# Reordering the opening stage of a two-block transformer kernel: loads, squares, first weights and PSUM banks

## The chip, the cores and the metric

The kernel runs on one NeuronCore of one Trainium2 chip. The core has five engines with a queue of instructions each: TensorE (PE in the profile, with its weight loads as PEld), VectorE (DVE), ScalarE (ACT), GpSimd (POOL) and SyncE (SP, which here only issues DMAs). Each queue runs in its own order and waits on semaphores of the others. The metric is the device time of one execution in microseconds; less is better.

## The reference, cut to what matters

Two transformer blocks run one after the other on one sequence of 512 tokens of width 1024, all in float32. What concerns the opening stage is the modulated norm at the entry of block 1, its first two projections, and the keys and values of a 256-row memory, which block 2 needs much later but which depend on nothing in block 1.

```python
mod = c @ w_ada + b_ada                                  # c is one row of 1024
shift, scale, gate = jnp.split(mod, 3, axis=-1)
h = _rmsnorm(x, norm_g) * (1.0 + scale[:, None, :]) + shift[:, None, :]
proj = h @ w_in                                          # q_a, k_a, v_a, z_a, q_b, ...
...
kv = jnp.einsum("bmd,de->bme", rmsnorm(mem, norm_mem_g), w_ckv)   # in block 2's cross attention
```

## The kernel before

**Number format.** Every large product is float32 built from three matmuls: weights and activations are split into a high part (fp32r) and a low part (the rest). For a weight tile of 128 x 1024 that is a cast on ScalarE (L166, `wh`) and a subtraction on VectorE or GpSimd (L167, `wl`); a string of letters (`START_LO`, D or P for each unit) says which. A "unit" is such a tile, 0.5 MiB in memory; it is loaded into `wr` (three buffers), and its two halves go into `wh` and `wl` (three buffers each).

**The front.** The first stage stands in a block whose order is written out by hand for all engines (`manual_schedule`): each engine runs its instructions in the order of the code. A loop over n = 0 to 9 runs ten units of the memory's keys (n = 0 to 7) and values (8, 9) on TensorE, 24 matmuls of 256 columns each, while block 1's input is prepared beside them. Around each unit stand: the squares of x (`squares_x`: ScalarE squares, one engine adds into `xacc`), the loads and the products of the modulation (`ada_load` reads one of 16 rows of tiles `ar`, and `ada` multiplies it with the broadcast row c in PSUM, `cb`, and sums along the row on VectorE; ScalarE then makes `shift` or `gain` of it), the copy of a finished unit to `kvo` and from there to DRAM by a DMA of the GpSimd queue, and some matmuls on zeros (`spin`, counts in `SPINS`). At n = `NORM_AT` the column sums of `xacc` give the norm's factor: a short chain on VectorE and ScalarE (`rsq`, `bcast_split`), then a broadcast on TensorE into `xrb` (PSUM).

**The eight h tiles.** `token_h(j)` makes one 128 x 512 slice of block 1's input: `y` = x times gain times `xrb` on VectorE into a PSUM bank, its high part on ScalarE (with the shift as bias), its low part on VectorE. `H_AT` says after which n slice j comes. Before, all eight y share one bank (tag `idle`).

**Queues.** SyncE issues all loads. A load of `wr` waits until the unit three before it has been split; a load of `ar` (eight buffers) waits until the product eight before it is done; and each issue waits for the DMA eight before it to have landed. Behind the loop stand `memory_squares` (the norm of the memory) and eight stores of the memory's split (`ms_d`).

**After the front.** From block 1 on the order is made by a list scheduler from the program's order. Block 1 opens with `qk("qa", "ka", 0)`: two chunks of 24 matmuls of 512 columns with the weights of units qa:0 and ka:0 and all eight h slices, then four units of values (va, into the banks `z` and `lin`).

Of the kernel before, what the change touches and what calls it, by code (L numbers as in the profile page):

```python
# [17 lines left out]
P = 128  # L18
# [3 lines left out]
KD = 8  # L22
# [53 lines left out]

START_LO = "DDDPPPPPPP"
N_FRONT = 10  # L80
AR_BUFS = 8
SQ_AT = (0, 0, 1, 1, 2, 2, 3, 3)
ADA_LOADS = (2, 2, 2, 2, 2, 2)
ADA_AT = (1, 1, 2, 2, 3, 3, 4, 4, 5, 5, 6, 6, 7, 7, 8, 8)
NORM_AT = 4
H_AT = (6, 6, 7, 7, 8, 8, 9, 9)
SPINS = (0, 2, 2, 2, 2, 3, 3, 3, 3, 3)
B1_LO = "DP"
B2_LO = 23 * "P" + "DPPDPDPDPDP"

# [25 lines left out]
def block_kernel(ctx, tc, wts, vec, c_row, lam_v, cst, x_t, mem_t, pos, out):  # L116
# [53 lines left out]
    def unit(name, j, n=D):  # L170
        return split(load(UNITS[name] + j, n), n)
# [13 lines left out]
    def chunk(name, c, xs, ps_=None):  # L185
        o = (ps_ or ps_lin)()
        lin_k(o, unit(name, c), 0, xs)
        return o

    def tok(name, xs, parts=(0,), ps_=None):  # L190
# [181 lines left out]
    def memory_squares():  # L372
        for raw in raws:
            act.activation(out=raw, in_=raw, func=AF.Square)
        s = raws[0]
        dve.tensor_tensor(out=s, in0=s, in1=raws[1], op=ALU.add)
        dve.tensor_tensor(out=s[:, :T], in0=s[:, :T], in1=s[:, T:], op=ALU.add)
        dve.tensor_tensor(out=mrb, in0=s[:, :NM], in1=s[:, NM:T], op=ALU.add)

    raw_of, split_of = {}, {}

    def mem_load(n):
        if n < N_FRONT:
            raw_of[n] = load(UNITS["mk"] + n)

    def mem_split(n):
        if n < N_FRONT:
# [55 lines left out]
    def ada(i):  # L445
        r, j, m = ada_raw[i], i // 2, mod[:, i:i + 1]
        dve.scalar_tensor_tensor(out=r, in0=r, scalar=1.0, in1=cb, op0=ALU.mult, op1=ALU.mult, accum_out=m)
        if i % 2 == 0:
            act.activation(out=shift[:, j:j + 1], in_=m, func=AF.Identity, bias=V("b_shift", j))
        else:  # L450
            act.activation(out=gain[:, j:j + 1], in_=m, func=AF.Identity, scale=V("norm_g", j),
                           bias=gain0[:, j:j + 1])
# [4 lines left out]
    def squares_x(i):  # L457
        if i == 0:
            act.activation(out=xacc, in_=xt0[:, 0], func=AF.Square)
            return  # L460
        q = st.tile([P, T], F32, tag="xq", bufs=3, name="xq")
        act.activation(out=q, in_=xt0[:, i], func=AF.Square)
        dve.tensor_tensor(out=xacc, in0=xacc, in1=q, op=ALU.add)

    def token_h(j):

        sh = shift[:, j:j + 1]
        y = stp.tile([P, T], F32, tag="idle", bufs=1, name="y")
# [8 lines left out]
    with tc.manual_schedule(engines={E_.PE, E_.Activation, E_.DVE, E_.Pool, E_.SP}):  # L477
# [15 lines left out]
        memory(1)  # L493
        mem_load(0)
        mem_load(1)
        for k in range(0, KD, 2):
            load_x(k)
        mem_load(2)
        for _ in range(4):
            ada_load()  # L500
        mem_split(0)
        mem_split(1)
        spun[0] = ps_sm()
        rest = []
        for n in range(N_FRONT):
# [6 lines left out]
            mem_split(n + 2)  # L512
            out_ = mem_unit(n)
            spin(SPINS[n])
            if n == NORM_AT:
                for i in range(NT):
                    pe.matmul(xrb[:, i:i + 1], lhsT=xacc[:, i * P:(i + 1) * P], rhs=ones[:, 0:1], start=True, stop=True)
                rsq(xrc, xrb[:, :NT], D)
                xrs = bcast_split(xrc)
            if n == NORM_AT + 1:  # L520
                bcast_mm(xrs, xrb)
            for i in range(16):
                if ADA_AT[i] == n:
                    ada(i)
                    if rest:
                        rest.pop()()
            out_()
            for j in range(KD):
                if H_AT[j] == n:
                    while rest:  # L530
                        rest.pop()()
                    rest.append(token_h(j))
        rest.pop()()
        memory_squares()
        for i, t in enumerate(mt):
# [128 lines left out]

    def qk(qn, kn, c):
        qe, qo, ke, ko, kl = qkt = qk_tiles(ap, lows)
        q_stack(chunk(qn, c, hs), 0.125, qe, qo)
        k_stack(chunk(kn, c, hs), ke, ko, kl)
        return qkt

    def head_out(v, p, odd, tt, zs):
# [926 lines left out]
```

## Time and profile before

| | us |
|---|---|
| three runs, median (lowest to highest) | 1288.9 (1286.59 to 1288.98) |
| the profiled execution, device time | 1287.82 |
| its span, first to last instruction | 1286.0 |
| TensorE busy in the span | 1225.6 |
| mean granted clock of TensorE | 0.978 |

The profiled execution took 1287.82 us, of which 1.8 us lie outside the span of instructions; it stands 1.1 us below the median. Times below count from the span's start. A row of the timeline gives start and length in microseconds, engine, line, operation, output and inputs, how many instructions it merges, and in brackets the idle time of the engine ahead of it and what ended that. A row of windows gives the busy time of each engine in a stretch, the mean granted clock of TensorE (1.00 is the upper of its two levels, 2.4 GHz; 0.5 the lower, 1.2 GHz), the busy share of the DMA engines and the rate.

### The profile page before, as it was taken

Reading aid. Unit: us, or ns where it says so; the run is one execution under the profiler, and the core shown is the slowest. Engines: PE = TensorE matmul, PEld = TensorE weight load, DVE = VectorE, ACT = ScalarE, POOL = GpSimd, SP = SyncE. Lnnn points to the kernel's source line nnn. Section 1 sums busy time; section 2 is a strip of 40 time slices with the busy share of each in tenths; the row PEclk is TensorE's granted clock in tenths of the full one; section 3 lists DMA queues with packets and bytes.
Section 4 is the critical chain, followed back from the end, with each engine's and each line's share of the span. In section 5 each row is a group of like instructions: output and inputs, shape, how many; then the busy total and the mean of one; then the engine's idle time right before and its main releaser. Section 6 shows DMA issues by size and latency. Waiting matters only on the chain. (4 is left out here: it accounts for less than half of the span.)

```text
span 1286.0 us, 16873 instructions
## 1 busy us (share of the span) xinstructions
PE 1225.6 (95%) x6381; PEld 1031.9 (80%) x6381; DVE 779.6 (61%) x1242; ACT 599.4 (47%) x989; POOL 451.6 (35%) x302
## 2 busy tenths in 40 slices
PE   7899999999999999999988888999999999999997
PEld 5688888988887888888877776887888888888886
DVE  5865778665564274457767867456587777771113
ACT  4456565556633345256555355444444444442222
POOL 1463444322222238334635446104422222222221
PEclk8989999999999999999998998999999999999999
DMA  9833222232257343221342324212233333322222
GB/s 357 328 120 110 87 74 81 67 90 74 83 175 249 107 124 98 66 90 42 101 139 68 102 77 131 97 34 81 84 97 98 99 99 98 99 90 90 90 90 66
DMA packets 46018, 140.10 MB, mean 109 GB/s; under 512 B 5233, under 2 KB 8817, under 8 KB 45938
## 3 DMA queue, kind: packets, MB, share of 16 engines
q1 hardware_dynamic: 45170, 136.93, 33.2%
q0 software_dynamic: 768, 2.10, 0.4%
q8 instruction: 50, 0.82, 0.3%
q14 instruction: 30, 0.25, 0.1%
HBM read 127.48 MB, written 8.39 MB: 106 GB/s over the span
## 5 line engine op out<-in xcount | busy, mean ns | idle before, releaser
L148 PE MATMUL lin<-h,wh 128*128 128x512 f32 (+1 forms) x2232 | 693.5, 391 | 17.2 <-ACT wh L166 13.8
L148 PEld LDWEIGHTS lin<-h,wh 128*128 128x128 f32 x2232 | 417.7, 192 | 102.6 <-ACT wh L166 17.6
L148 PE MATMUL lin<-h,wl 128*128 128x512 f32 (+1 forms) x1116 | 434.7, 390 | 11.5 <-POOL wl L167 8.8
L167 POOL TENSOR_TENSOR wl<-wr,wh 128x1024 fp32r<-128x1024 f32 (+1 forms) x115 | 277.7, 2416 | 473.6 <-ACT wh L166 449.7
L166 ACT CAST wh<-wr 128x1024 fp32r<-128x1024 f32 (+1 forms) x197 | 204.6, 1040 | 255.0 <-PE lin L148 183.8
L148 PEld LDWEIGHTS lin<-h,wl 128*128 128x128 f32 x1116 | 214.2, 192 | 55.8 <-POOL wl L167 11.0
L167 DVE TENSOR_TENSOR wl<-wr,wh 128x1024 fp32r<-128x1024 f32 (+1 forms) x82 | 111.6, 1361 | 127.8 <-ACT wh L166 127.4
L148 PE MATMUL lin<-wh,h 128*128 128x256 f32 x672 | 128.8, 288 | 2.3 <-DVE h L1010 2.3
L148 PEld LDWEIGHTS lin<-wh,h 128*128 128x128 f32 x672 | 107.6, 193 | 3.1 <-issue 2.7
L1383 DVE SCALAR_TENSOR_TENSOR cv<-up,vecs,cv 128x512 f32<-128x512 f32 x88 | 94.2, 1071 | 18.3 <-ACT cv L1381 16.8
L148 PE MATMUL lin<-wl,h 128*128 128x256 f32 x336 | 96.1, 286 | 0.4 <-POOL wl L167 0.4
L148 PE MATMUL lin<-zz,wh 128*128 128x512 f32 (+1 forms) x324 | 92.3, 371 | 0.0
L148 PEld LDWEIGHTS lin<-zz,wh 128*128 128x128 f32 x324 | 58.5, 188 | 11.5
L148 PEld LDWEIGHTS lin<-wl,h 128*128 128x128 f32 x336 | 65.0, 194 | 1.0 <-POOL wl L167 0.7
L148 PE MATMUL lin<-zz,wl 128*128 128x512 f32 (+1 forms) x162 | 60.1, 371 | 0.0
L321 POOL TENSOR_TENSOR nacc<-nacc,sq 128x512 f32<-128x512 f32 x34 | 53.0, 1568 | 14.9 <-ACT sq L320 14.3
L1378 POOL MEMSET up<- 128x2 f32 x44 | 4.3, 99 | 148.5 <-DVE cv L1383 116.3
L683 POOL TENSOR_TENSOR zs<-zs,y 64x512 f32<-64x512 f32 x16 | 26.5, 1654 | 71.4 <-DVE y L682 69.8
L697 DVE TENSOR_TENSOR_SCAN om<-om 128x511 f32<-128x511 f32 (+3 forms) x32 | 35.9, 1162 | 9.5 <-ACT om L693 9.4
L1390 ACT ACTIVATE cv<-cv 128x512 f32<-128x512 f32 x22 | 13.9, 632 | 59.6 <-DVE cv L1383 59.6
L1379 DVE TENSOR_TENSOR up<-lin,rb 128x512 f32<-128x512 f32 x44 | 30.1, 686 | 16.1 <-PE lin L148 13.4
L218 DVE TENSOR_TENSOR tl<-z,th 128x512 fp32r<-128x512 f32 (+1 forms) x60 | 33.4, 595 | 9.5 <-ACT th L217 9.1
(406 smaller groups left out, 1715.6 us busy)
## 6 DMA issues: line engine op xcount, KB each, us to landing
wr<-in_wts SPq DMA_DIRECT2D x197, 512.0 KB, 3.5
ar<-in_wts SPq DMA_DIRECT2D x16, 512.0 KB, 9.4
qk<-qk SPq DMA_DIRECT2D x24, 128.0 KB, 2.3
wr<-in_wts SPq DMA_DIRECT2D x8, 384.0 KB, 3.0
xt<-in_x_t SPq DMA_DIRECT2D x4, 512.0 KB, 8.9
kv_d<-kvo POOLq DMA_DIRECT2D x16, 128.0 KB, 4.9
ms_d<-h SPq DMA_DIRECT2D x8, 256.0 KB, 6.2
ma_d<-gt SPq DMA_DIRECT2D x8, 256.0 KB, 4.0
```

The lines of the kernel that those rows point to most:

```text
L148: pe.matmul(o, lhsT=lhsT, rhs=rhs, start=start, stop=stop, skip_group_check=True)
L166: act.copy(out=hi[:, :n], in_=raw[:, :n])
L167: lo_engine().tensor_tensor(out=lo[:, :n], in0=raw[:, :n], in1=f32(hi[:, :n]), op=ALU.subtract)
L218: dve.tensor_tensor(out=lo, in0=src, in1=f32(hi), op=ALU.subtract)
L321: pool.tensor_tensor(out=acc, in0=acc, in1=q, op=ALU.add)
L683: pool.tensor_tensor(out=zs[r], in0=zs[r], in1=y[r], op=ALU.mult)
L697: dve.tensor_tensor_scan(out=om[:, o:e], data0=om[:, o:e], data1=om[:, o:e], initial=1.0, op0=ALU.mult, op1=ALU.bypass)
L1378: pool.memset(up[:, T:], 0.0)
L1379: dve.tensor_tensor(out=up[:, :T], in0=o, in1=rb[:, 0], op=ALU.mult)
L1383: dve.scalar_tensor_tensor(out=r, in0=up[:, 2 - j:2 - j + T], scalar=V("ffn_w", c * 3 + j), in1=r, op0=ALU.mult, op1=ALU.add)
L1390: act.activation(out=a, in_=a, func=AF.Silu)
```

## The change

All of it lies in the front and in the first call of block 1.

- **Loads.** SyncE's order is new: two modulation rows come ahead of x, and the others between the four loads of x and the units, where before all of x came first.
- **Products earlier.** `ADA_AT` moves the 16 products forward (three ahead of the loop), and their small ScalarE steps come one iteration after the product, collected in `acts`.
- **Squares.** The adds into `xacc` and the three adds of `memory_squares` move from VectorE to GpSimd. All squares come at n = 0 and 1.
- **Norm and h earlier.** `NORM_AT` is 3 for 4, and h starts after n = 5 for 6.
- **Two banks for y.** Odd j takes a bank of tag `lin`, even j keeps `idle`; the low part of slice j comes after the y of slice j+1.
- **qa:0 and ka:0 inside the front.** Their loads and splits become numbers 10 and 11 of the front's own order, ahead of the `ms_d` stores, and `qk` takes them from there.
- **Small.** Unit 2 is split with GpSimd and unit 3 with VectorE (before the other way round); the counts of zero matmuls are 2 where they were 3.

```diff
-START_LO = "DDDPPPPPPP"
+START_LO = "DDPDPPPPPPPP"
-SQ_AT = (0, 0, 1, 1, 2, 2, 3, 3)
-ADA_LOADS = (2, 2, 2, 2, 2, 2)
-ADA_AT = (1, 1, 2, 2, 3, 3, 4, 4, 5, 5, 6, 6, 7, 7, 8, 8)
-NORM_AT = 4
-H_AT = (6, 6, 7, 7, 8, 8, 9, 9)
-SPINS = (0, 2, 2, 2, 2, 3, 3, 3, 3, 3)
+SQ_AT = (0, 0, 0, 0, 1, 1, 1, 1)
+ADA_LOADS = (1, 2, 2, 2, 1)
+ADA_AT = (-1, -1, -1, 0, 0, 1, 1, 2, 2, 3, 3, 4, 4, 5, 5, 6)
+NORM_AT = 3
+H_AT = (5, 5, 6, 6, 7, 7, 8, 8)
+SPINS = (0, 2, 2, 2, 2, 2, 2, 2, 2, 2)
...
-        dve.tensor_tensor(out=s, in0=s, in1=raws[1], op=ALU.add)
-        dve.tensor_tensor(out=s[:, :T], in0=s[:, :T], in1=s[:, T:], op=ALU.add)
-        dve.tensor_tensor(out=mrb, in0=s[:, :NM], in1=s[:, NM:T], op=ALU.add)
+        pool.tensor_tensor(out=s, in0=s, in1=raws[1], op=ALU.add)
+        pool.tensor_tensor(out=s[:, :T], in0=s[:, :T], in1=s[:, T:], op=ALU.add)
+        pool.tensor_tensor(out=mrb, in0=s[:, :NM], in1=s[:, NM:T], op=ALU.add)
...
-        if n < N_FRONT:
-            raw_of[n] = load(UNITS["mk"] + n)
+        if n < N_FRONT + 2:
+            raw_of[n] = load(UNITS["mk"] + n if n < N_FRONT else UNITS[("qa", "ka")[n - N_FRONT]])
...
-        dve.tensor_tensor(out=xacc, in0=xacc, in1=q, op=ALU.add)
+        pool.tensor_tensor(out=xacc, in0=xacc, in1=q, op=ALU.add)
...
-        y = stp.tile([P, T], F32, tag="idle", bufs=1, name="y")
+        y = ps_lin() if j % 2 else stp.tile([P, T], F32, tag="idle", bufs=1, name="y")
...
-        for k in range(0, KD, 2):
-            load_x(k)
+        ada_load()
+        ada_load()
+        load_x(0)
+        ada_load()
+        load_x(2)
         mem_load(2)
-        for _ in range(4):
-            ada_load()
+        ada_load()
+        load_x(4)
+        ada_load()
+        load_x(6)
         mem_split(0)
+        ada_load()
         mem_split(1)
+        ada_load()
+        ada_load()
...
                 if H_AT[j] == n:
-                    while rest:
-                        rest.pop()()
                     rest.append(token_h(j))
+                    if len(rest) > 1:
+                        rest.pop(0)()
...
+        wq, wk = (split_of.pop(N_FRONT + e) if N_FRONT + e in split_of else None for e in range(2))
+        q_stack(chunk(qn, c, hs, w=wq), 0.125, qe, qo)
+        k_stack(chunk(kn, c, hs, w=wk), ke, ko, kl)
```

SyncE's order of loads, before (`wr` are units, `xt` is x in two tiles a load, `ar` the modulation's rows, `ms_d` the stores of the memory's split):

```order
5 L153 DMA wr<-in_wts 128x1024 x2
6 L455 DMA xt_83<-in_x_t 128x2x512 x4
7 L153 DMA wr<-in_wts 128x1024
8 L442 DMA ar<-in_wts 128x1024 x4
9 L153 DMA wr<-in_wts 128x1024 x2
10 L442 DMA ar<-in_wts 128x1024 x2
```

and the same place of the changed kernel:

```order
5 L153 DMA wr<-in_wts 128x1024 x2
6 L442 DMA ar<-in_wts 128x1024 x2
7 L454 DMA xt_83<-in_x_t 128x2x512
8 L442 DMA ar<-in_wts 128x1024
9 L454 DMA xt_83<-in_x_t 128x2x512
10 L153 DMA wr<-in_wts 128x1024
11 L442 DMA ar<-in_wts 128x1024
12 L454 DMA xt_83<-in_x_t 128x2x512
13 L442 DMA ar<-in_wts 128x1024
14 L454 DMA xt_83<-in_x_t 128x2x512
15 L153 DMA wr<-in_wts 128x1024
```

Counted in loads behind the first unit's, the first modulation row moves from 7th to 2nd, the fifth from 13th to 10th, the fourth unit from 11th to 12th.

VectorE from the last of the short norm chain on, before (`ar,mod` is a modulation product; `h<-y` a low part):

```order
22 L298 TENSOR_TENSOR bcl<-xrc,bch 128x4
23 L447 SCALAR_TENSOR_TENSOR ar,mod<-ar,cb 128x1024 x6
24 L469 SCALAR_TENSOR_TENSOR y<-xt_83,gain,xrb 128x512
25 L473 SCALAR_TENSOR_TENSOR h<-y,shift,h 128x512
26 L469 SCALAR_TENSOR_TENSOR y<-xt_83,gain,xrb 128x512
27 L447 SCALAR_TENSOR_TENSOR ar,mod<-ar,cb 128x1024
28 L473 SCALAR_TENSOR_TENSOR h<-y,shift,h 128x512
29 L447 SCALAR_TENSOR_TENSOR ar,mod<-ar,cb 128x1024
```

and after:

```order
17 L298 TENSOR_TENSOR bcl<-xrc,bch 128x4
18 L447 SCALAR_TENSOR_TENSOR ar,mod<-ar,cb 128x1024 x4
19 L468 SCALAR_TENSOR_TENSOR y<-xt_83,gain,xrb 128x512
20 L468 SCALAR_TENSOR_TENSOR lin<-xt_83,gain,xrb 128x512
21 L472 SCALAR_TENSOR_TENSOR h<-y,shift,h 128x512
22 L447 SCALAR_TENSOR_TENSOR ar,mod<-ar,cb 128x1024
23 L549 CAST msb<-csts 128x128
24 L468 SCALAR_TENSOR_TENSOR y<-xt_83,gain,xrb 128x512
```

Eleven products stand ahead of the norm chain instead of six, one behind the first y instead of four, and two y stand ahead of the first low part.

GpSimd at the end of the front, before (`mr`, `mrb` are the memory's squares, `selr` a constant of block 1):

```order
20 L167 TENSOR_TENSOR wl<-wr,wh 128x1024
21 L429 DMA kv_d<-kvo 128x256
22 L167 TENSOR_TENSOR wl<-wr,wh 128x1024
23 L418 DMA kv_d<-kvo 128x256 x2
24 L167 TENSOR_TENSOR wl<-wr,wh 128x1024 x2
25 L631 TENSOR_SCALAR selr<-wr 128x1024
```

and after:

```order
22 L167 TENSOR_TENSOR wl<-wr,wh 128x1024
23 L429 DMA kv_d<-kvo 128x256
24 L167 TENSOR_TENSOR wl<-wr,wh 128x1024 x2
25 L418 DMA kv_d<-kvo 128x256 x2
26 L376 TENSOR_TENSOR mr<-mr 128x1024
27 L167 TENSOR_TENSOR wl<-wr,wh 128x1024 x2
28 L377 TENSOR_TENSOR mr<-mr 128x512
29 L378 TENSOR_TENSOR mrb<-mr 128x256
30 L167 TENSOR_TENSOR wl<-wr,wh 128x1024
```

The splits of qa:0 and ka:0 stand ahead of the last two `kv_d` issues, and the memory's adds now stand between the splits of the values' units.

## Rows read from the trace of the kernel before

**Rows 1.** The page, busy time and share of the span.

```profile
PE 1225.6 (95%) x6381; PEld 1031.9 (80%) x6381; DVE 779.6 (61%) x1242; ACT 599.4 (47%) x989; POOL 451.6 (35%) x302
```

**Rows 2.** Windows: stretch and its length, busy of five engines, clock, DMA, rate.

```profile
20.00:60.00 40.00, 33.37 (x226) 29.46 (x225) 31.61 (x49) 17.80 (x38) 20.27 (x14) 0.91 1.00 375
60.00:67.50 7.50, 2.07 (x11) 0.98 (x9) 6.06 (x12) 4.47 (x8) 2.73 (x2) 0.86 0.18 73
67.50:80.30 12.80, 12.72 (x46) 10.39 (x47) 7.42 (x10) 7.75 (x10) 8.38 (x6) 0.81 0.41 117
80.30:400.00 319.70, 317.05 (x1773) 269.07 (x1773) 210.05 (x359) 175.61 (x317) 109.78 (x68) 0.99 0.34 103
```

**Rows 3.** Timeline of TensorE, from the last unit to the values' first matmul.

```profile
60.52 0.82 PE L345 MATMUL sm<-zeros 128*128 128x512 bf16 x3
64.74 0.73 PE L148 MATMUL lin<-h,wh 128*128 128x512 f32 x2 [3.40 <-ACT wh L166]
67.58 1.22 PE L148 MATMUL lin<-h,wh 128*128 128x512 f32 x2 [2.11 <-ACT wh L166]
...
75.60 0.61 PE L148 MATMUL lin<-h,wh 128*128 128x512 f32 x2
...
80.36 0.40 PE L148 MATMUL z<-wh,h 128*128 128x256 f32 x2
```

**Rows 4.** Timeline of VectorE, 26 to 72 us.

```profile
26.64 4.61 DVE L463 TENSOR_TENSOR xacc<-xacc,xq 128x512 f32<-128x512 f32 x2 [3.17 <-ACT xq L462]
...
40.51 2.14 DVE L267 TENSOR_TENSOR rq<-xrc 128x4 f32<-128x4 f32 x1
...
50.43 0.75 DVE L469 SCALAR_TENSOR_TENSOR y<-xt,gain,xrb 128x512 f32<-128x512 f32 x1
51.93 0.75 DVE L473 SCALAR_TENSOR_TENSOR h<-y,shift,h 128x512 fp32r<-128x512 f32 x1 [0.76 <-ACT h L471]
52.72 0.76 DVE L469 SCALAR_TENSOR_TENSOR y<-xt,gain,xrb 128x512 f32<-128x512 f32 x1
53.38 1.21 DVE L447 SCALAR_TENSOR_TENSOR ar<-ar,cb 128x1024 f32<-128x1024 f32 x1
...
70.86 0.75 DVE L473 SCALAR_TENSOR_TENSOR h<-y,shift,h 128x512 fp32r<-128x512 f32 x1 [0.81 <-ACT h L471]
```

**Rows 5.** Timeline of ScalarE: unit casts, three of them ended by a landing.

```profile
10.81 1.04 ACT L166 CAST wh<-wr 128x1024 fp32r<-128x1024 f32 x1 [0.25 <-DMA wr<-in_wts]
...
17.48 1.05 ACT L166 CAST wh<-wr 128x1024 fp32r<-128x1024 f32 x1 [4.19 <-DMA wr<-in_wts]
...
24.30 1.04 ACT L166 CAST wh<-wr 128x1024 fp32r<-128x1024 f32 x1 [4.45 <-DMA wr<-in_wts]
...
63.06 0.69 ACT L471 ACTIVATE h<-y,shift 128x512 fp32r<-128x512 f32 x1 [0.34 <-DVE y L469]
63.65 1.03 ACT L166 CAST wh<-wr 128x1024 fp32r<-128x1024 f32 x1
```

**Rows 6.** Timeline of GpSimd: three unit splits and two DMA issues.

```profile
28.31 2.38 POOL L167 TENSOR_TENSOR wl<-wr,wh 128x1024 fp32r<-128x1024 f32 x1
...
40.25 2.37 POOL L167 TENSOR_TENSOR wl<-wr,wh 128x1024 fp32r<-128x1024 f32 x1 [0.18 <-ACT wh L166]
...
64.77 2.35 POOL L167 TENSOR_TENSOR wl<-wr,wh 128x1024 fp32r<-128x1024 f32 x1 [6.67 <-ACT wh L166]
67.08 1.09 POOL L418 DMA_DIRECT2D kv_d<-kvo  x2
```

**Rows 7.** Timeline of TensorE: a unit's steps at the lower and the upper clock.

```profile
28.14 0.63 PE L148 MATMUL lin<-h,wh 128*128 128x256 f32 x2
...
28.79 0.63 PE L148 MATMUL lin<-h,wh 128*128 128x256 f32 x2
...
33.22 0.40 PE L148 MATMUL lin<-h,wh 128*128 128x256 f32 x2
...
33.57 0.40 PE L148 MATMUL lin<-h,wh 128*128 128x256 f32 x2
```

**Rows 8.** The page's groups: out<-in, count, busy us, mean ns, idle before.

```profile
L321 POOL TENSOR_TENSOR nacc<-nacc,sq 128x512 f32<-128x512 f32 x34 | 53.0, 1568 | 14.9 <-ACT sq L320 14.3
```

More of the change, by code (lines that the diff above doesn't have):

```diff
@@ L183, in lin_k, with chunk @@
             mm3(o, wh[:, c], wl[:, c], xh, xl, start and j == 0, stop and j == n - 1)
-    def chunk(name, c, xs, ps_=None):
+    def chunk(name, c, xs, ps_=None, w=None):
         o = (ps_ or ps_lin)()
-        lin_k(o, unit(name, c), 0, xs)
+        lin_k(o, w or unit(name, c), 0, xs)
         return o
@@ L375, in memory_squares @@
         s = raws[0]
-        dve.tensor_tensor(out=s, in0=s, in1=raws[1], op=ALU.add)
-        dve.tensor_tensor(out=s[:, :T], in0=s[:, :T], in1=s[:, T:], op=ALU.add)
-        dve.tensor_tensor(out=mrb, in0=s[:, :NM], in1=s[:, NM:T], op=ALU.add)
+        pool.tensor_tensor(out=s, in0=s, in1=raws[1], op=ALU.add)
+        pool.tensor_tensor(out=s[:, :T], in0=s[:, :T], in1=s[:, T:], op=ALU.add)
+        pool.tensor_tensor(out=mrb, in0=s[:, :NM], in1=s[:, NM:T], op=ALU.add)
     raw_of, split_of = {}, {}
     def mem_load(n):
-        if n < N_FRONT:
-            raw_of[n] = load(UNITS["mk"] + n)
+        if n < N_FRONT + 2:
+            raw_of[n] = load(UNITS["mk"] + n if n < N_FRONT else UNITS[("qa", "ka")[n - N_FRONT]])
     def mem_split(n):
-        if n < N_FRONT:
+        if n < N_FRONT + 2:
             lo_seq[:] = START_LO[n], -1
@@ L448, in ada @@
         if i % 2 == 0:
[L449 to L452, printed above, removed]
+            return lambda: act.activation(out=shift[:, j:j + 1], in_=m, func=AF.Identity, bias=V("b_shift", j))
+        return lambda: act.activation(out=gain[:, j:j + 1], in_=m, func=AF.Identity, scale=V("norm_g", j),
+                                      bias=gain0[:, j:j + 1])
     def load_x(k):
@@ L495, in block_kernel @@
         mem_load(1)
-        for k in range(0, KD, 2):
-            load_x(k)
+        ada_load()
[3 more added lines that the diff above has]
+        load_x(2)
         mem_load(2)
-        for _ in range(4):
-            ada_load()
+        ada_load()
+        load_x(4)
+        ada_load()
+        load_x(6)
         mem_split(0)
+        ada_load()
         mem_split(1)
+        ada_load()
+        ada_load()
         spun[0] = ps_sm()
         rest = []
+        acts = [ada(i) for i in range(16) if ADA_AT[i] < 0]
         for n in range(N_FRONT):
@@ L512, in block_kernel @@
             mem_split(n + 2)
+            while acts:
+                acts.pop(0)()
             out_ = mem_unit(n)
@@ L517, in block_kernel @@
                     pe.matmul(xrb[:, i:i + 1], lhsT=xacc[:, i * P:(i + 1) * P], rhs=ones[:, 0:1], start=True, stop=True)
+            for i in range(16):
+                if ADA_AT[i] == n:
+                    acts.append(ada(i))
+            if n == NORM_AT:
                 rsq(xrc, xrb[:, :NT], D)
@@ L521, in block_kernel @@
                 bcast_mm(xrs, xrb)
[L522 to L525, printed above, removed]
-                        rest.pop()()
             out_()
@@ L529, in block_kernel @@
                 if H_AT[j] == n:
-                    while rest:
-                        rest.pop()()
                     rest.append(token_h(j))
+                    if len(rest) > 1:
+                        rest.pop(0)()
         rest.pop()()
@@ L666, in qk @@
         qe, qo, ke, ko, kl = qkt = qk_tiles(ap, lows)
-        q_stack(chunk(qn, c, hs), 0.125, qe, qo)
-        k_stack(chunk(kn, c, hs), ke, ko, kl)
+        wq, wk = (split_of.pop(N_FRONT + e) if N_FRONT + e in split_of else None for e in range(2))
+        q_stack(chunk(qn, c, hs, w=wq), 0.125, qe, qo)
+        k_stack(chunk(kn, c, hs, w=wk), ke, ko, kl)
         return qkt
```

## The prediction, made before the changed kernel had run

> **What bounds the kernel now.** I read the page first: TensorE is busy 1225.6 of 1286.0 us, no other engine over 61% [rows 1]. So what counts is when TensorE idles or runs slowly. The windows say where that is for this change: from 80.3 to 400 us, which is block 1 and a little of block 2, it is busy 317.05 of 319.70 us at clock 0.99 [rows 2], so whatever the front gives back arrives at the end of the kernel as a shift, if block 1 keeps its supply. In 20 to 60 us the DMA engines are busy all the time (share 1.00, 375 GB/s) [rows 2]; then their share falls to 0.18 while TensorE does 2.07 us of work in 7.5 us. The loads have ended and something else is late.
>
> TensorE's timeline names it. The last unit's zero matmuls end at 60.52 + 0.82 = 61.3 us, then come waits of 3.40 and 2.11 us, both for the cast of unit qa:0 on ScalarE or what hangs on it, and the values' first matmul starts at 80.36 us [rows 3]. Between lie the two chunks qa:0 and ka:0, 48 matmuls. At the upper clock 7 steps of 3 matmuls took 80.36 - 75.60 = 4.76 us, 0.227 us each [rows 3], so 48 are 10.9 us. From 61.3 to 80.36 are 19.0 us: **8.1 us lost**, to the waits and to the lower clock that follows them (0.81 in that window [rows 2]).
>
> Why it is late stands on VectorE and ScalarE. With one bank for y, each h slice goes y 0.75, a wait of 0.76 for ScalarE, low part 0.75: 52.72 - 50.43 = 2.3 us, with products of 1.14 us pitch between, and the eighth low part ends at 70.86 + 0.75 = 71.6 us [rows 4]. The cast of qa:0 stands behind the fifth slice in ScalarE's queue, at 63.65 us [rows 5], and GpSimd's half of it starts at 64.77 [rows 6]. VectorE's head start was lost before that: six products ran back to back behind the norm chain.
>
> **The change, part by part.** I walk the new order forward with durations of rows.
>
> *Loads.* Behind the second unit's landing (10.81 us) five loads of 0.5 MiB took until 17.48, the next five until 24.30 [rows 5]: 1.33 and 1.36 us, mean 1.35. The fifteenth modulation row (the last that slices 0 and 1 stand behind) is the 25th load behind that unit in the new order: 10.8 + 25 x 1.35 = 44.5 us. Four `kv_d` stores of 128 KB share the engines by then, a quarter load each, +1.3: **45.8 us**. The 375 GB/s of 20 to 60 us, stores included, give 1.40 a load and the same 45.8. Bytes are unchanged; only the order is. The eleventh row, which the norm chain stands behind, is the 19th load: 36.5 + 1.0 = 37.5 us. SyncE's waits for buffers (a split of the unit three before, a product eight before) come 4 to 7 us ahead of the queue running dry, so they cost nothing; if a split were later than that, its delay is added whole.
>
> *Against a page.* The rows show 375 GB/s over 40 us. The Trainium skill, "DMA: Bandwidth & Descriptors", section Specifications, gives about 358 GB/s of HBM for one core; by it the loads behind the first 20 us would land some 1 us later and the gain be 1 us less. The trace is above that figure, and I go by the trace.
>
> *Squares on GpSimd.* Seven adds at 1.57 us [rows 8], 11 us of GpSimd. On VectorE an operation of this size takes 0.75 us, but two of these adds cost 4.61 us beside GpSimd's split that started at 28.31 [rows 4, 6]. The adds run from 16 to 31 us, around unit 2's split (21.5 to 23.9); the norm chain wants the sum only behind the eleventh product, 37.5 + 1.1 = 38.6 us. Cover: 7 us. Without it each add costs 0.8 us more than on a free VectorE. Unit 3's split, now on VectorE at about 28 us, may stand behind an add or two (2 to 3 us); its unit then ends on TensorE by 37 us and still precedes the chain.
>
> *Norm chain.* Its second step took 2.14 us because GpSimd's split of 40.25 to 42.62 was running; the same kind of step on so few elements is done in a fraction of that [rows 4, 6]. In the new order GpSimd then stands at a `kv_d` issue behind ScalarE's copy, which comes after the chain, so it is idle: chain 38.6 to 40.4, broadcast on TensorE to 41.5. If it is caught again, +2.
>
> *h slices.* The first y starts when VectorE has done product 15: 45.8 + 1.14 = 47.0 us, 3.4 us ahead of before. With two banks VectorE no longer waits: 16 steps at about 0.70 (0.66 from y to the next instruction [rows 4]), product 16 at 1.14, two small casts 0.3: 12.6 us, last low part at **59.6 us** instead of 71.6.
>
> *The units on TensorE.* A step of a unit takes 0.65 us at the lower clock, 0.36 at the upper [rows 7]; eight steps 5.2 or 2.9. Unit 9's weights are the last link: its cast stands in ScalarE's queue behind slice 3 (y done at 52.8, high part 53.5), so cast to 54.5, GpSimd 2.4 to 56.9, unit 9 from 57.0 to 59.9, zero matmuls to **60.4 us**. Unit 5 starts at 41.5 and even at the lower clock ends by 46.7, unit 6 to 8 follow by 56.4, so TensorE itself is just in time. qa:0: cast behind slice 5 to 57.2, GpSimd to 59.6; ka:0 to 62.3, wanted at 65.9. So qa:0 starts at 60.4 with weights and slices ready, and the values start at 60.4 + 10.9 = **71.3 us**, against 80.36: a gain of 9.0 us. Of it 8.1 are the lost stretch, 0.9 an earlier end of the units.
>
> *What then is late.* GpSimd has the memory's adds now: two `kv_d` issues 1.1 [rows 6], adds 2.4 and, with unit splits between, 1.6 and 0.8 (half of 1.6, an estimate). Splits of the four value units end at 68.2, 70.6, 75.4 and, behind `selr` and four memsets, 82.8; TensorE wants them at 71.3, 77.1, 82.8 and 88.6. Cover 3 us at the first; each microsecond beyond that is paid. The eight `ms_d` stores now stand ahead of the values' loads, 2 MiB, 5.4 us, done by 59; the first value load waits for qa:0's split (59.6) anyway. The list scheduler's order of block 1 shifts a little; block 1 idles 2.65 us before, so this can give at most that back, and I bound a loss by the same amount.
>
> *Sum.* 1287.8 (the profiled execution) - 9.0 = 1278.8. That execution stands 1.1 below the median, from which the same step gives 1279.9; I take **1279.3**. Bounds of the unknown terms: loads at 1.33 without the stores' share +1.8 of gain; block 1 +-2.65; chain caught and a unit at the lower clock -2 to -4.
>
> **The rivals.**
>
> *A, half of it.* The engines' queues couple: ScalarE's copies of finished units stand ahead of the next slices' high parts and casts, so a late TensorE makes ScalarE late, then GpSimd, then TensorE again. One lower-clock unit (2.3) plus one caught chain or add (2) are then paid: gain 4 to 5, about **1283.8**. For it: waits of units for GpSimd were there before [rows 3, 5]. Against: 5 us of cover in the early units. The share that GpSimd's extra 11 us of adds becomes the bound belongs here.
>
> *B, more.* Loads land early and block 1 loses its idle time: 9 + 1.8 + 1.5, **1276**.
>
> *C, hidden.* The front's end moves but a supply behind it (value units on GpSimd, their loads behind the stores) holds TensorE near its old times: within 0.2%, some **1287**. For it: GpSimd's queue in 60 to 75 us is nearly full in my walk. Against: 3 us and more of cover at each unit.
>
> *D, slower.* TensorE falls to the lower clock at every short wait of the front and stays there, since there are fewer zero matmuls. Five units (5 to 9) at the lower clock cost 5 x 2.3 = 11.5, and the first chunk 2.2 more [rows 7, 2]: 13.7 - 9.0 = 4.7 late, **1293**. It turns slower when four of the five units stay low. For it: the clock of 20 to 60 us is 0.91 already [rows 2]. Against: in the front it came back within one unit after each wait (lower at 28.14, upper at 33.22 [rows 7]).
>
> **How the numbers follow.** Forecast 0.58 (1277.0 to 1281.5), A 0.20, B 0.10, C 0.06, D 0.06. The range holds the forecast, A and half of B: 1275.8 to 1284.8. A measurement of this kernel can tell about 0.2% (2.6 us) from no change: faster means under 1286.3. That gives faster 0.88, same 0.07, slower 0.05 (of C and D, a little of C to either side).
>
> **What would show it.** In the changed kernel's trace the values' first matmul should start at 70 to 72.5 us, the first y at 45 to 47.5, the last low part at 58 to 60, with a pitch near 1.4 a slice; qa:0 should start without waits at the upper clock; the norm chain should have no step over 0.5 us; GpSimd should finish the adds by 32. Wrong would be: a first y after 50 us (loads), idle time of TensorE for GpSimd's splits in 50 to 75 us, or a window of 80 to 390 us with more than 4 us of idle TensorE (scheduler).

## The result, and the profile of the changed kernel

| | before | changed |
|---|---|---|
| median (lowest to highest, six runs each) | 1287.96 us (1286.59 to 1288.98) | 1279.78 us (1277.78 to 1283.41) |
| profiled execution, its span | 1287.82 us, 1286.0 us | 1280.37 us, 1278.6 us |
| values' first matmul | 80.36 us | 73.86 us |

The ratio is 0.9939 (95% interval 0.9922 to 0.9956): faster by 8.2 us between the medians, by 7.45 between the two profiled executions. The prediction had said 1279.3, and 9.0 us between the profiled executions. One execution of the kernel squares_dve below took 3081.61 us and is left out of its median.

Units and slices of h are counted from 0, as in the code, products of the modulation from 1.

The page's busy time, which answers [rows 1]: TensorE has 3.6 us less of it, and the span 7.4 us less.

```profile
PE 1222.0 (96%) x6371; PEld 1029.0 (80%) x6376; DVE 765.8 (60%) x1232; ACT 603.2 (47%) x992; POOL 465.7 (36%) x312
```

Four windows of the changed kernel (stretch and length, busy us of TensorE, its weight loads, VectorE, ScalarE, GpSimd, granted clock, DMA share, GB/s), against [rows 2]. In 60 to 67.5 us TensorE is now busy for 7.43 us instead of 2.07, at the upper clock: the lost stretch of the old front is closed. But in 20 to 60 us it is busy for 29.22 us instead of 33.37. In the window of block 1 it is idle for 2.2 us.

```profile
20.00:60.00 40.00, 29.22 (x197) 26.64 (x201) 30.75 (x51) 21.01 (x43) 28.63 (x21) 0.91 0.96 362
60.00:67.50 7.50, 7.43 (x44) 6.50 (x44) 1.04 (x2) 4.89 (x6) 6.69 (x5) 1.00 0.91 278
67.50:71.30 3.80, 3.80 (x18) 3.16 (x17) 0.00 (x0) 1.06 (x1) 3.34 (x3) 1.00 0.17 66
80.30:391.00 310.70, 308.48 (x1717) 261.05 (x1716) 201.03 (x355) 176.07 (x316) 102.53 (x65) 1.00 0.32 99
```

TensorE's timeline (start, us, line, operation, idle time before it and what ended it), against [rows 3]. The qa chunk now starts at 62.74 without a wait, and the values follow 11.1 us later at 73.86. What is new stands ahead of that: unit 8 (`lin<-wh,h`) waits 2.54 us for ScalarE's copy of unit 7's result to `kvo`. In the list of waits of the kernel before, no wait of TensorE is for a `kvo`.

```profile
40.25 0.33 PE L148 MATMUL xrb<-identr,bch 128*128 128x128 f32 x1 [4.13 <-ACT bch L297]
...
50.08 0.51 PE L148 MATMUL lin<-h,wh 128*128 128x256 f32 x2 [0.43 <-ACT kvo L428]
...
53.28 0.38 PE L345 MATMUL sm<-zeros 128*128 128x512 bf16 x1
56.20 0.38 PE L148 MATMUL lin<-wh,h 128*128 128x256 f32 x1 [2.54 <-ACT kvo L428]
...
62.74 0.81 PE L148 MATMUL lin<-h,wh 128*128 128x512 f32 x2
...
73.86 0.52 PE L148 MATMUL z<-wh,h 128*128 128x256 f32 x3
```

VectorE's timeline, against [rows 4]: the eleventh product waits for its row until 37.42, the step of the norm chain that took 2.14 us takes 0.16, the first y starts at 46.23. Then one operation is out of place: a cast of 128x128 constants takes 2.29 us at 49.54, and the third y waits behind it until 51.76. The last low part starts at 60.45.

```profile
37.42 1.22 DVE L447 SCALAR_TENSOR_TENSOR ar<-ar,cb 128x1024 f32<-128x1024 f32 x1 [0.29 <-DMA ar<-in_wts]
...
39.21 0.16 DVE L267 TENSOR_TENSOR rq<-xrc 128x4 f32<-128x4 f32 x1
...
46.23 0.75 DVE L468 SCALAR_TENSOR_TENSOR y<-xt,gain,xrb 128x512 f32<-128x512 f32 x1
...
49.54 2.29 DVE L549 CAST msb<-csts 128x128 bf16<-128x128 f32 x1
51.76 0.74 DVE L468 SCALAR_TENSOR_TENSOR y<-xt,gain,xrb 128x512 f32<-128x512 f32 x1
...
60.45 0.75 DVE L472 SCALAR_TENSOR_TENSOR h<-lin,shift,h 128x512 fp32r<-128x512 f32 x1 [0.17 <-ACT h L470]
```

GpSimd's timeline, against [rows 6], shows what ran beside that cast: a unit's split from 49.39 to 51.76. The cast, at 51.83, ends with it. GpSimd's last four adds end at 29.67.

```profile
23.40 6.27 POOL L462 TENSOR_TENSOR xacc<-xacc,xq 128x512 f32<-128x512 f32 x4
...
49.39 2.37 POOL L167 TENSOR_TENSOR wl<-wr,wh 128x1024 fp32r<-128x1024 f32 x1 [2.09 <-ACT wh L166]
```

ScalarE's timeline, against [rows 5], shows why unit 7's copy came so late. Unit 7 had ended at 53.3. Its copy stood in the queue behind slice 3's high part, which waited for the delayed y, behind unit 9's cast and behind a gain.

```profile
53.99 0.69 ACT L470 ACTIVATE h<-lin,shift 128x512 fp32r<-128x512 f32 x1 [0.77 <-DVE lin L468]
54.57 1.03 ACT L166 CAST wh<-wr 128x1024 fp32r<-128x1024 f32 x1
55.51 0.39 ACT L450 ACTIVATE gain<-mod,gain,vecs 128x1 f32<-128x1 f32 x1
55.80 0.36 ACT L428 COPY kvo<-lin 128x256 f32<-128x256 f32 x1
```

Behind the front, two rows of the source view of each kernel tell the rest. Such a row gives the shortest, median and longest duration in ns and the first and last start of a line's operations; the changed kernel's lines stand ten further down. At `h<-lin,ro`, early in block 2, the changed kernel is 526.1 - 517.7 = 8.4 us ahead; at `z<-ones,nacc` it is 743.5 - 736.1 = 7.4 us ahead, and so it is at the end.

```profile
L1010 DVE TENSOR_TENSOR h<-lin,ro x8: 211/212/215, 526.1 to 620.9; 128x64 f32<-128x64 f32 x8
L1110 PE MATMUL z<-ones,nacc x8: 250/250/271, 743.5 to 744.3; 128*128 128x1 f32 x8
```

```profile
L1020 DVE TENSOR_TENSOR h<-lin,ro x8: 211/214/215, 517.7 to 612.6; 128x64 f32<-128x64 f32 x8
L1120 PE MATMUL z<-ones,nacc x8: 250/250/271, 736.1 to 736.9; 128*128 128x1 f32 x8
```

So the 7.4 us are: front 6.5, another 1.9 by the row of `h<-lin,ro`, and 1.0 lost again in block 2. The 1.9 are a difference. Two waits of the kernel before are gone, 0.38 us at 393.54 and 1.77 us in the row below, with the lower clock that followed it for some 3.5 us (1.05 us for a pair of matmuls instead of 0.61 [rows 3], so about 0.42 of those 3.5, or 1.5 us). Against that, waits for `p` grew from 0.5 to 1.7, and one of 0.39 for `tl` is new. Together that is 2.1, near the 1.9. TensorE in the kernel before:

```profile
396.03 0.50 PE L148 MATMUL lin<-h,wl 128*128 128x512 f32 x1 [1.77 <-POOL wl L167]
...
397.46 1.05 PE L148 MATMUL lin<-h,wh 128*128 128x512 f32 x2
```

The 1.9 do not come from the front's earlier end. In every kernel of the next section but spins0 the `h<-lin,ro` row starts 443.6 to 444.0 us behind the values' first matmul, against 445.7 in the kernel before; that holds for old_loads too, whose front ends no earlier than before. So they belong to something that all these kernels share and no experiment undid, such as loading and splitting qa:0 and ka:0 in the front or the memory's adds on GpSimd. Which of these it is was not tested. The row in old_loads (values at 80.39):

```profile
L1020 DVE TENSOR_TENSOR h<-lin,ro x8: 214/215/216, 524.2 to 619.0; 128x64 f32<-128x64 f32 x8
```

The 1.0 is lost at one place, shown at the end of the next section.

### The profile page after: what moved, and what is told of

It is laid out like the page before. It is cut to its first block, busy times and chain, and to the rows that moved or that the text cites. A ratio compares the mean times of both kernels' runs of the same rounds, so it can differ in the third digit from the quotient of the medians.

```text
span 1278.6 us, 16838 instructions
## 1 busy us (share of the span) xinstructions
PE 1222.0 (96%) x6371; PEld 1029.0 (80%) x6376; DVE 765.8 (60%) x1232; ACT 603.2 (47%) x992; POOL 465.7 (36%) x312
```

## The experiments

All times in the table are of the profiled execution, but for the median. "First y" and "values" are the starts of the first y on VectorE and of the values' first matmul on TensorE. The last column is the ratio to the kernel before, run on the same chip. Each kernel was profiled once; the medians are of 3 to 10 executions, and those of the changed kernel alone span 5.6 us.

| kernel | first y | values | span | median | ratio (95%) |
|---|---|---|---|---|---|
| before | 50.43 | 80.36 | 1286.0 | 1287.96 | 1 |
| changed | 46.23 | 73.86 | 1278.6 | 1279.78 | 0.9939 (0.9922, 0.9956) |
| copy_first | 45.95 | 72.66 | 1277.0 | 1278.84 | 0.9935 (0.9915, 0.9955) |
| casts_late | 46.39 | 71.68 | 1276.5 | 1278.07 | 0.9923 (0.9903, 0.9944) |
| both | 46.23 | 71.39 | 1276.2 | 1277.73 | 0.9922 (0.9898, 0.9946) |
| one_bank | 46.72 | 75.27 | 1280.8 | 1281.02 | 0.9948 (0.9931, 0.9965) |
| old_loads | 53.77 | 80.39 | 1285.5 | 1286.58 | 1.0000 (0.9991, 1.0009) |
| x_first | 46.24 | 73.87 | 1279.2 | 1281.05 | 0.9951 (0.9937, 0.9965) |
| squares_dve | 45.79 | 74.90 | 1279.8 | 1280.29 | 0.9956 (0.9940, 0.9973) |
| qaka_last | 46.37 | 75.52 | 1280.4 | 1282.14 | 0.9968 (0.9955, 0.9981) |
| spins0 | 46.12 | 72.87 | 1278.9 | 1280.71 | 0.9959 (0.9944, 0.9973) |
| casts_squares | 46.69 | 71.98 | 1275.8 | 1277.73 | 0.9925 (0.9910, 0.9940) |
| casts_qaka | 45.99 | 71.44 | 1275.8 | 1277.62 | 0.9927 (0.9913, 0.9940) |
| units_first | 46.33 | 72.98 | 1278.0 | 1279.75 | 0.9940 (0.9928, 0.9953) |

Apart from old_loads, the first y of the kernels with the new order lies within 45.8 to 46.7: differences of half a microsecond at that point are not taken for an effect of an edit.

### The copy ahead of the cast (copy_first)

```
-            mem_split(n + 2)
+            mem_split(n + 2) if n != 7 else None
...
-            out_()
+            out_(), mem_split(n + 2) if n == 7 else None
```

> Only the place of unit 9's weight cast on ScalarE changes: it stands behind the copy of unit 7's result instead of ahead of it. Theory (units wait for a PSUM bank): in the changed kernel unit 7 ends at 53.3 us on TensorE, its bank is copied out only at 55.80 because slice 3's high part (53.99), the cast for unit 9 (54.57, 1.03) and a gain stand ahead, and unit 8 waits 2.54 us for it. With the copy ahead of the cast it is done by 55.2, unit 8 starts near 55.1, the wait falls to about 1.4; the cast and GpSimd's half for unit 9 come 0.4 later (58.5), so unit 9 starts at 58.6 instead of 59.44 and the values at 73.0 instead of 73.86: 0.8 us earlier. Rival 1 (the chain of slices and weights holds the end, the bank does not): values at 73.9 to 74.3. Rival 2 (unit 8 waits for something else that came at the same time): the wait of 2.5 us stays. Median against the changed kernel: -0.8 by the theory, 0 to +0.4 by the rivals.

Measured: values at 72.66, 1.2 us earlier, of which 0.3 were there at the first y. Timelines of ScalarE and TensorE:

```profile
54.58 0.36 ACT L428 COPY kvo<-lin 128x256 f32<-128x256 f32 x1
```

```profile
54.99 0.38 PE L148 MATMUL lin<-wh,h 128*128 128x256 f32 x1 [1.21 <-ACT kvo L428]
```

Unit 8 starts 0.05 us behind the end of the copy, in this order as in the changed kernel's: the wait is for it, and both rivals fall.

### The casts of constants behind the front (casts_late)

The load of `csts` moves with them.

```
         memory_squares()
+        dve.tensor_copy(out=identb, in_=ident)
+        dve.tensor_copy(out=msb, in_=C("msb"))
+        dve.tensor_copy(out=mfox, in_=C("mfox"))
...
-    dve.tensor_copy(out=identb, in_=ident)
-    dve.tensor_copy(out=msb, in_=C("msb"))
-    dve.tensor_copy(out=mfox, in_=C("mfox"))
```

> The three small casts of constants on VectorE (0.2 us each when alone) and their load stand behind the front's last low part instead of between products and slices. Theory (port): the first of them took 2.29 us at 49.54 only because GpSimd's split ran from 49.39 to 51.76; slices and products, which are operations of another kind, ran beside such splits at their usual 0.75. Without it the third y starts at 49.6 instead of 51.76, the last low part at about 58.2 instead of 60.45, the high part of slice 3 and the cast for unit 9 come 2.2 us earlier, unit 8 waits under 1 us, and the values start at 71.3 to 71.7 instead of 73.86. Rival 1 (the block moves to the next VectorE operation that runs beside the split): the third y or a low part takes over 2 us and the values start at 73.5 to 74. Rival 2 (the slices are not what holds the front's end): the third y is early and the values still start at 73.5 to 74. Median against the changed kernel: -2.2 to -2.5 by the theory, 0 by the rivals.

Measured: values at 71.68, as the theory had it. VectorE's, GpSimd's and TensorE's timelines of this kernel:

```profile
49.70 0.75 DVE L468 SCALAR_TENSOR_TENSOR y<-xt,gain,xrb 128x512 f32<-128x512 f32 x1
...
58.27 0.75 DVE L472 SCALAR_TENSOR_TENSOR h<-lin,shift,h 128x512 fp32r<-128x512 f32 x1 [0.17 <-ACT h L470]
...
59.07 0.22 DVE L547 CAST msb<-csts 128x128 bf16<-128x128 f32 x1
```

```profile
49.55 2.38 POOL L167 TENSOR_TENSOR wl<-wr,wh 128x1024 fp32r<-128x1024 f32 x1 [1.80 <-ACT wh L166]
```

```profile
54.02 0.39 PE L148 MATMUL lin<-wh,h 128*128 128x256 f32 x1 [0.18 <-ACT kvo L428]
...
60.56 0.81 PE L148 MATMUL lin<-h,wh 128*128 128x512 f32 x2
...
71.68 0.52 PE L148 MATMUL z<-wh,h 128*128 128x256 f32 x3
```

The same cast takes 0.22 us where no split runs. The third y, at 49.70, ran its whole 0.75 us beside a split (49.55 to 51.93 here) and was not held, though it started as shortly behind the split's start as the cast had in the changed kernel (0.15 us both times). So whether an operation is held is a matter of its kind. The Trainium skill, "SBUF — State Buffer", section "Who interferes with whom", has a rule for it: VectorE and GpSimd share a pair of ports that one instruction holds to its end, a cast can need it, depending on its operands, and an instruction with at most one input from SBUF, outside the two-port modes, doesn't. The trace agrees with that rule, with 2.29 against 0.22 us for the cast and 0.75 for a y, whose second tensor stands in PSUM.

### Both edits (both)

> Both edits together: casts of constants behind the front, unit 7's copy ahead of unit 9's cast. By the two theories they are one chain, not two: with slice 3's high part at about 51.8 the queue of ScalarE is free before unit 7 ends at 53.3, so the copy is in time with either order, and the second edit only makes the cast for unit 9 wait for unit 7 (53.3 + 0.4, GpSimd to 57.2). So values at 71.3 to 71.8, no better than the casts alone. Rival (two separate costs that add): 0.8 us better than the casts alone, values at 70.5.

Measured: values at 71.39, 0.3 us ahead of the casts alone and not 0.8 or more. The stalled cast and the bank wait were one chain: the cast made the slice late, the slice made the copy late, the copy held unit 8.

### One bank for y (one_bank)

```
-        y = ps_lin() if j % 2 else stp.tile([P, T], F32, tag="idle", bufs=1, name="y")
+        y = stp.tile([P, T], F32, tag="idle", bufs=1, name="y")
...
-                    if len(rest) > 1:
+                    if len(rest) > 0:
...
-        rest.pop()()
```

> Undoes one part: each y stands in the same PSUM bank again, so each low part follows its own slice before the next y. Loads, squares, first weights stay as in the changed kernel. Theory: each slice then costs VectorE 0.75, a wait of 0.76 for ScalarE, 0.75, i.e. 2.3 us instead of 1.4; from a first y at 46.2 the last low part starts near 66, the cast for unit 9 behind slice 3 comes at about 57, its GpSimd half at 60.5, unit 9 ends at 63.5, the qa weights behind slice 5 are ready near 64, and the values start at 75 to 76.5, i.e. 1.2 to 2.6 us later than the 73.86 of the changed kernel; the units no longer share their banks with y, so the wait for unit 7's copy is gone. Rival 1 (banks cost the units as much as the slices gain): values at 73.5 to 74. Rival 2 (the second bank carries most of the front's gain): values at 78 or later.

Measured: values at 75.27, inside the theory's range. Unit 8 on TensorE, and unit 7's copy on ScalarE:

```profile
53.74 0.47 PE L148 MATMUL lin<-wh,h 128*128 128x256 f32 x1
```

```profile
57.25 0.36 ACT L428 COPY kvo<-lin 128x256 f32<-128x256 f32 x1
```

With no y in the units' banks unit 8 starts 3.5 us ahead of unit 7's copy. That shows what it waited for in the changed kernel: a bank. The second bank is worth 1.4 us net at the values' start, although it takes each slice from 2.3 to 1.4 us. (The cast of constants happened to miss the split in this kernel and took 0.23 us instead of 2.29, which favours this kernel; by how much at the values' start was not tried.)

### The old order of loads (old_loads)

```
-ADA_LOADS = (1, 2, 2, 2, 1)
+ADA_LOADS = (2, 2, 2, 2, 2, 2)
...
+        for k in range(0, KD, 2):
+            load_x(k)
         mem_load(2)
+        for _ in range(4):
+            ada_load()
         mem_split(0)
         mem_split(1)
```

> Undoes one part: the front's loads in the order of the kernel before (x first, then four modulation rows, then two rows between the units' weights); operations on all other engines keep the changed kernel's order. Theory (the 25th load decides): the fifteenth modulation row is the 27th load behind the second unit's again, and the eleventh the 21st, so at 1.35 us a load both land 2.7 us later: norm chain from 41.2 instead of 38.57, first y at 48.9 instead of 46.23. The rest of the front follows, values at 75.5 to 76.6 instead of 73.86; a little less if the constants' cast no longer meets a split of GpSimd. Rival 1 (the units on TensorE hold the front's end, the rows have slack): first y late but values at 73.5 to 74.3. Rival 2 (rows early in the front matter most, since VectorE then stands at products while weights wait): values at 78 or later.

Measured: values at 80.39, and a median of 1286.58 against 1286.54 for the kernel before on the same chip: the whole gain is gone. Rival 2 has the size, but not the reason. The norm chain came at 41.75, near the forecast 41.2; the first y came at 53.77 instead of 48.9. SyncE's issues, then GpSimd's split and ScalarE's cast:

```profile
37.43 0.33 SPq L153 DMA_DIRECT2D wr<-in_wts  x1
37.80 0.98 SPq L442 DMA_DIRECT2D ar<-in_wts  x2
47.09 0.33 SPq L153 DMA_DIRECT2D wr<-in_wts  x1
47.51 0.86 SPq L442 DMA_DIRECT2D ar<-in_wts  x2
```

```profile
44.69 2.38 POOL L167 TENSOR_TENSOR wl<-wr,wh 128x1024 fp32r<-128x1024 f32 x1 [0.18 <-ACT wh L166]
```

```profile
43.55 1.05 ACT L166 CAST wh<-wr 128x1024 fp32r<-128x1024 f32 x1
```

```profile
52.62 1.22 DVE L447 SCALAR_TENSOR_TENSOR ar<-ar,cb 128x1024 f32<-128x1024 f32 x1 [5.63 <-DMA ar<-in_wts]
```

The last two modulation rows stand in SyncE's queue behind a weight load. That load needs a buffer which GpSimd's split frees at 47.07, and the split's cast stands on ScalarE behind the norm chain. So the rows are issued at 47.51, the DMA engines run dry (busy share 0.00 in 46 to 48 us), and the fifteenth product starts at 52.62, with the first y right behind it. In the changed kernel the last row is issued at 38.53. The kernel before had this order of loads too, but only twelve products ahead of its first y (50.43): so the new order of products has its part in making a late fifteenth row this dear.

### x first, the tail as changed (x_first)

The front's first ten loads go back to their old order (x ahead of all rows); nothing else changes.

> Only the first ten loads change: x stands ahead of all modulation rows again instead of between them; from the tenth load on the order is the changed kernel's, so the modulation rows still end two loads earlier than in the kernel before. The run with the whole old load order lost 6.5 us at the values' start. Theory (the tail of the rows decides): there the last two rows stood in SyncE's queue behind a weight load that waited for a buffer until 47.09 us and were issued at 47.51; here they stand ahead of it, so first y at 46.2 +-0.5 and values at 73.4 to 74.6, as in the changed kernel. Rival (the interleaved start makes the gain, VectorE never makes up for products that begin 6 us later): norm chain at 40 or later, first y at 48.5 or later, values at 76 or later.

Measured: first y 46.24, values 73.87, against 46.23 and 73.86. Of the new order of loads, the interleaving of x and modulation rows does nothing here; what counts is that no row is left behind the weight load that waits for the chain. (Its median is 1.3 us above the changed kernel's all the same, with intervals that overlap: so much can two medians differ without a difference in the front.)

### Squares on VectorE (squares_dve, casts_squares)

```
-        pool.tensor_tensor(out=xacc, in0=xacc, in1=q, op=ALU.add)
+        dve.tensor_tensor(out=xacc, in0=xacc, in1=q, op=ALU.add)
```

> Undoes one part: the seven adds of x squares on VectorE again, everything else as in the changed kernel. Theory (hidden): VectorE stands at loads until 43.8 us and takes the seven adds (0.75 us each, up to 2.4 where a GpSimd split runs beside) in that slack; GpSimd is 11 us freer and unit 2's wait of 2.91 us for its split falls below 1; the norm chain is held by the eleventh row's load at 37.4 either way, so first y at 46.2 +-0.5 and values at 73.6 to 74.2: no change. Rival (the adds hold VectorE's products back, as they did in the kernel before): first y at 47.5 or later and values at 75 to 76.

Measured: first y at 45.79, as the theory had it, yet values at 74.90, outside it. TensorE's timeline shows another cause, unit 8's steps (three matmuls each) behind the bank wait:

```profile
55.78 0.58 PE L148 MATMUL lin<-wh,h 128*128 128x256 f32 x1 [2.56 <-ACT kvo L428]
...
56.37 0.63 PE L148 MATMUL lin<-wh,h 128*128 128x256 f32 x2
```

A pair of matmuls takes 0.63 us, the lower clock; in the changed kernel, behind a wait of 2.54, it took 0.40. A step then takes 0.64 us instead of 0.36, and five of them cost 1.4 us. So the edit was repeated on top of casts_late, where the wait is 0.2 us:

> On top of the kernel with the constants' casts behind the front: x squares added on VectorE again instead of GpSimd. In the run that undid this alone the first y came 0.44 us earlier, yet the values came 1.04 later, with five steps of unit 8 at the lower clock behind its bank wait. Theory (the adds are hidden on either engine, the clock after the long bank wait made the difference): with the bank wait gone, first y at 45.8 to 46.3 and values at 71.1 to 71.9 against 71.68. Rival (GpSimd's adds are worth 1 us): values at 72.5 to 73.

Measured: values at 71.98, a little past the theory's 71.1 to 71.9 and 0.3 us behind casts_late, as its first y was (46.69 against 46.39). The rival's 72.5 to 73 did not come: the adds are hidden on either engine in this order.

### qa and ka behind the last slice (qaka_last, casts_qaka)

The casts of qa and ka move from behind slices 5 and 7 to behind slice 7, both.

> Moves one part: block 1's first weights (qa, ka) are still loaded early, but their casts on ScalarE stand behind the last slice's high part instead of behind the sixth and the eighth. Theory (the place decides): the cast of qa starts at 60.4 instead of 57.33, GpSimd's half ends at 63.9 instead of 61.0, TensorE, which starts qa at 62.74, waits about 0.7 us for it and may drop to the lower clock for two steps; ka's half ends at 66.3, before it is wanted. Values at 74.6 to 75.2 instead of 73.86. Rival 1 (these weights have slack): values at 73.7 to 74.0. Rival 2 (a wait there costs as much as in the kernel before, where waits and lower clock together cost 8 us): values at 77 or later.

Measured: values at 75.52, outside all three ranges, but the qa chunk did not wait; again unit 8 ran five steps at the lower clock behind its bank wait (2.31 us) and ended late. That decides nothing, so the edit was repeated on top of casts_late:

> On top of the kernel with the constants' casts behind the front: the casts of qa and ka stand behind the last slice's high part. Undone alone, this could not be read, since unit 8 ran five steps at the lower clock and the weights came in time for it. Theory (the place decides once the slices are early): with the casts' stall gone the last high part ends at 58.3, the cast of qa at 59.3, GpSimd's half at 61.8, against a unit 9 that ends at 60.3; TensorE can do four matmuls with the high half (0.9 us) and waits 0.4 to 1.0 us, ka is in time. Values at 72.1 to 72.7 against 71.68. Rival 1 (slack): 71.5 to 71.9. Rival 2 (the wait brings the lower clock and cascades): 73.5 or later.

Measured: values at 71.44, rival 1 (slack). TensorE's timeline of casts_qaka:

```profile
60.17 1.28 PE L148 MATMUL lin<-h,wh 128*128 128x512 f32 x4
61.35 0.51 PE L148 MATMUL lin<-h,wl 128*128 128x512 f32 x1
```

Four matmuls with the high half cover the time until GpSimd's half is there. The exact place of these casts has slack. What the two units would cost outside the front's order was not tried, since that reorders block 1; so how much of the front's 6.5 us hangs on having them in the front is not shown.

### No zero matmuls (spins0)

`SPINS = (0, 0, 0, 0, 0, 0, 0, 0, 0, 0)`

> The zero matmuls between the front's units are left out (they compute nothing that is used). Theory (units at the upper clock follow from the units' own work, and short waits are made good within a unit): values at 73.5 to 74.6 instead of 73.86, the granted clock of 41 to 63 us at 0.88 to 0.95 against 0.93. Rival (rival D of the prediction: without them TensorE drops to the lower clock at each short wait and stays there): granted clock under 0.75 in 41 to 63 us, units of 5.2 us instead of 2.9, and values at 77 to 83.

Measured: values at 72.87, granted clock in 41.6 to 62.7 us 0.93 as in the changed kernel: rival D falls. In 20 to 41.6 us the clock was 0.75 instead of 0.91, where the units have cover. The 1.0 us gained was lost again, and 0.7 more, by the `h<-lin,ro` row (518.4 against 517.7). That goes with a stretch at clock 0.98 (172.9 to 272.9 us) where the changed kernel has 1.00: behind the same waits for `p` a pair of matmuls takes 1.05 us at 199.49.

### Unit 5 ahead of the broadcast (units_first)

```
-            if n == NORM_AT + 1:
+            if n == NORM_AT + 2:
                 bcast_mm(xrs, xrb)
```

> The two edits of the run with both (constants' casts behind the front, unit 7's copy ahead of unit 9's cast), and one more: on TensorE unit 5 stands ahead of the broadcast of the norm instead of behind it. Theory (with the slices early, the row of units on TensorE is the bound: it stands idle for 4.1 us at the norm chain, and unit 5 then runs its first four steps at the lower clock, while unit 5's weights are ready at 38.1): unit 5 runs from 38.2 instead of 41.6, the broadcast ends by 43.5, ahead of the first y at 46.2; unit 6 starts at 44.1 instead of 46.0, units 7 to 9 follow with GpSimd's halves, unit 9's at about 55.5, and the values start at 69.5 to 70.5 against 71.39; median 1.0 to 1.8 below the run with both (1277.7), 1276. Rival (slices and weights hold the end: unit 9's cast behind slices, GpSimd full): values at 71.0 to 71.5, no change.

Measured: values at 72.98, 1.6 us later than in the kernel both. The theory fell, and the rival's 71.0 to 71.5 was missed too. TensorE:

```profile
50.18 0.52 PE L148 MATMUL lin<-h,wh 128*128 128x256 f32 x2 [2.27 <-ACT kvo L428]
```

Unit 7, in this row, only waits longer for its bank (in both it waited 0.21 us at 50.08): unit 6's copy still stands behind slice 1's high part and unit 8's cast, until 50.1 in this kernel and 50.0 in the changed one. Behind the longer wait five steps ran at the lower clock (0.63 us for a pair from 50.71 on). So at this place it is the slices that set the pace, through ScalarE's queue, and not TensorE's row of units.

### Where block 2 loses 1.0 us

One TensorE row of before, and the same place in the changed kernel:

```profile
658.24 0.72 PE L148 MATMUL lin<-h,wh 128*128 128x512 f32 x2 [2.73 <-DVE cp L1023]
```

```profile
649.92 1.22 PE L148 MATMUL lin<-h,wh 128*128 128x512 f32 x2 [3.09 <-DVE cp L1033]
```

The wait is 0.36 us longer, and the clock is at its lower level from the first matmul on, where before it still ran one pair at the upper. The changed kernel is still 8.3 us ahead when the wait ends (658.24 - 649.92), so what is lost here is the slower steps behind it. The wait is 3.1 us in all experiments but the two with the squares on VectorE (2.9). Why it is longer than before was not tested.

## Why the prediction was right, and which steps were not

**The sum** came within 0.5 us of the median, and so close it came partly by luck. The front gave 6.5 us instead of 9.0; block 1 gave 1.9, taken as 0 with a bound of 2.65; block 2 took 1.0, which no term had. The median that the sum started from helped as well: 1288.9 over three executions became 1287.96 over six, so the forecast fall of the median was 9.6 us and the measured one 8.2. Two of the named signs were missed: the values' first matmul came at 73.86 (70 to 72.5 forecast), and the last low part ran from 60.45 to 61.2 (58 to 60).

**The casts.** The step that failed is "two small casts 0.3", within the 12.6 us from the first y to the last low part. They took 2.29 + 0.21 us. The prediction had read the block by GpSimd in [rows 4, 6] for the adds and the norm chain and bounded both; it did not ask which other VectorE operations of that kind the new order sets beside a split. casts_late shows that this is nearly all of the front's shortfall: without the stall the last low part starts at 58.27 (forecast end 59.6, measured 59.0), qa starts at 60.56 (60.4) and the values at 71.68 (71.3).

**The bank.** This was missed altogether: y in a `lin` bank makes the units share three banks with the slices, so a unit waits for an earlier unit's copy. Rival A had the coupling the other way round (copies hold the slices). It cost 2.5 us at unit 8, but only because the slices were late already; copy_first won 1.2 by itself and 0.3 with the casts moved.

**The loads** were forecast well (eleventh row 37.5, measured 37.42; first y 47.0, measured 46.23), by counting loads. old_loads shows that the count alone does not carry the gain: by it the values would have come at 75.5 to 76.6, and they came at 80.39. The sentence "if a split were later than that, its delay is added whole" was the important one: the rows must be out of SyncE's queue before a weight load waits for the chain. The prediction wrote 0.9 of 9.0 us down to an earlier end of the units and 8.1 to the lost stretch; without the loads' new tail all of the front's 6.5 are gone, in spite of two banks, the squares on GpSimd and early weights. These undos don't add up to shares, since the parts need each other.

**As forecast:** norm chain 38.6 to 40.4 without a caught step (38.57 to 40.39); GpSimd's adds done by 31 (29.67); GpSimd's value splits without a wait of TensorE; 48 matmuls of qa and ka 10.9 us (11.1), at the upper clock.

**Rivals.** C is out: the time won in the front arrived whole in block 2. D is out by the result, and by spins0, where even without zero matmuls the clock in 41.6 to 62.7 us was the same 0.93. Of A there was a part, by another mechanism. B did not come: the front gave less than forecast, not more.

**A better version.** The four kernels with the casts behind the front and the broadcast where it was have medians of 1277.6 to 1278.1, some 2 us under the changed kernel and 0.7 to 0.8% under the one before. Their intervals overlap that of the changed kernel, so the medians alone do not show the difference; the traces, all with the values 1.9 to 2.5 us earlier, agree with it.

## What to carry to other kernels

When an order is changed, walk each queue for what can wait in it, and for what stands behind that: here, with the old loads, a weight load that waited for a buffer held two unrelated loads in the same queue and cost the whole gain of the front. Where two engines block each other by kind of operation, list every operation of that kind near the critical chain, however small: a cast of 0.2 us cost 2.1. And a PSUM bank taken for one purpose is taken from another, so read the waits for releases along with the waits for data.

## What the runs showed of the hardware that was not expected

After waits of TensorE of about the same length, each behind a unit at the upper clock, the clock came back differently: behind 2.54, 2.55 and 3.01 us (changed, x_first, spins0) unit 8 ran at the upper clock, behind 2.56 and 2.31 us (squares_dve, qaka_last) five steps ran at the lower. Each kernel was traced once, so whether this goes with the kernel or with the execution is not shown. It is 1.4 us by which two traces with the same waits can differ, and more than most of the edits here were worth: an edit is better judged in a kernel where the wait is gone.
